# First products of a two-layer network: the making of their input chunks rewritten, norm sums reordered

## Chip, cores and metric

One Trainium2 chip, one core. The metric is the device time of one execution in microseconds, the median of several runs.

## What is computed

Two layers over 256 context and 256 latent tokens of width 1024, kept side by side as 512 columns. The modulation vectors come from `silu(cond) @ mod_w`, once with the latent's condition `c` and once with the context's. Cut to what the change touches:

```python
def ada_mod(cond, w, b):
    m = jax.nn.silu(cond) @ w + b
    return jnp.split(m[..., None, :], N_MOD, axis=-1)

mx = ada_mod(c, mod_w[i], mod_b[i]); mc = ada_mod(c_ctx, mod_w[i], mod_b[i])
x = x + 0.5 * mx[2] * swiglu(modulate(rms_norm(x, norm_g[i, 0]), mx[0], mx[1]),
                             ffn_w_in[i, 0], ffn_w_out[i, 0])      # the same for h_ctx with mc
# then a mixer (layer 0: gated linear recurrence, layer 1: retention), then a second swiglu
# modulate(h, shift, scale) = h * (1 + scale) + shift
```

At the end comes a last norm of the latent half alone.

## The kernel before

**Tiling.** Everything lies transposed: `x[k]` (k = 0..7) is a tile of 128 channels by 512 tokens, columns 0 to 255 context, 256 to 511 latent. The normed and modulated input of a product is `h[k]`, a high and a low part of 128x512 each (fp32r, a split of fp32 in two). Weights come as 371 tiles of 128x1024 (eight blocks of 128x128) in order of use; each is split by ScalarE (high part, L112) and VectorE (low part, L138). A block times a chunk is three matmuls (`mm3`, L142 to L144): high by high, high by low, low by high.

**Order.** The order of each engine's queue is that in which the program is written out (`manual_schedule`); an engine takes its queue in order. SP issues all transfers. Weight tiles are fetched up to four ahead and split two ahead of use (`w_ahead`, called from `w` at the first block of a tile; `w_low` emits the low part).

**Modulation.** `mods` lists 144 tiles of 128x1024, two vectors of 128 channels each (one for each condition). A tick (`_tick`) works off the next. In form V it is two VectorE multiplications with a sum (L242), in form P sixteen TensorE matmuls with two columns (L237). For layer 0, tiles 0, 2, 4, ... 14 are the shift of chunks 0 to 7 (form V), tiles 1, 3, ... 15 the scale (form P); `mod_finish` adds bias and norm gain in small VectorE steps (L262 to L265).

**Start.** `run` loads `cT`, `ident`, eight x tiles, two modulation tiles, the small vectors, then modulation and weight tiles in turn. Four fill matmuls (`warm`), then `spread_c` copies the conditions over all partitions with TensorE (L195). ScalarE squares the x tiles, VectorE adds them up (L286), `stat` (L296) sums over partitions on TensorE and computes the inverse root in ten small VectorE steps (L305 to L316), `bcast` (L329) spreads it. Tile 0 stands on VectorE between the sums and the ten steps, tile 1 on TensorE behind the sums, tiles 2 and 3 behind the broadcast. `h_chunk` makes an h: two VectorE steps (L346, one for each half), two ScalarE steps (L348), two VectorE steps for the low part (L354).

**First group.** `first_group` multiplies six column blocks (three pairs of the gated layer) by chunk 0, then by chunk 1 and so on, 18 matmuls for each chunk. A hook behind chunk k does the two ticks and the `h_chunk` of chunk k + 2. Behind chunk 7 comes `softplus_setup`, 29 small VectorE and two ScalarE steps. The gating (`post`, L485, L486, L157, L158) and the next pair of column blocks follow.

**The two ends with the latent half alone.** `boundary(x_only=True)` closes the retention and the last feed-forward layer: `out_proj` updates x chunk by chunk (L393) and squares it (`sq_acc`), VectorE adds the squares, then `stat`, ten fill matmuls, `bcast`, and, except at the very end, six more fill matmuls and two `h_chunk`s. The other four ends go half by half, with other products in between.

Of the kernel before, what the change touches and what calls it, by code (L numbers as in the profile page):

```python
# [9 lines left out]
F32 = mybir.dt.float32  # L10
# [6 lines left out]
P = 128  # L17
# [26 lines left out]
def mod_order():  # L44

    out = []
    for k in range(KD):
        out.append((0, 0, k, "V", True))
        out.append((0, 1, k, "P", True))
    for idx in range(2, 9):  # L50
        for k in range(KD):
            out.append((0, idx, k, "V", True))
    for idx in range(9):
        for k in range(KD):
            out.append((1, idx, k, "V", idx < 5))
    return out
# [18 lines left out]
class Kernel:  # L75
    def __init__(self, tc, aps):
        self.tc, self.nc, self.aps = tc, tc.nc, aps
        self.keys = []
        self.wt = {}
        self.raw = {}  # L80
        self.nsplit = 0
        self.wlow = deque()
        self.ndma = 0
        self.mods = mod_order()
        self.mod_done = 0
        self.mod_dma = 0
        self.mod_raw = {}
        self.mod_count = {}
        self.modpool = None
        self.hold = set()  # L90
        self.holdpool = None
        self.pend = []
        self.rate = 1
        self.bga, self.bgv = deque(), deque()

# [7 lines left out]

    def w_ahead(self, t):
        nc = self.nc
        self.w_fetch(min(t + LA + DA + 1, NTILES))
        while self.nsplit < min(t + LA + 1, NTILES):
            raw = self.raw.pop(self.nsplit)
            pool, tag = (self.holdpool, "h") if self.nsplit in self.hold else (self.wpool, "w")
            hi = pool.tile([P, BPT * P], F32R, tag=tag + "hi", name=tag + "hi", bufs=4)  # L110
            lo = pool.tile([P, BPT * P], F32R, tag=tag + "lo", name=tag + "lo", bufs=4)
            nc.scalar.activation(hi, raw, AF.Copy)  # L112
            self.wt[self.nsplit] = (hi, lo)
            self.wlow.append((lo, raw, hi))
            self.nsplit += 1

    def w(self, key, n=1):
# [6 lines left out]
        if o == 0:  # L124
            self.w_ahead(t)
            self.wt.pop(t - 2, None)
        if o >= 4 or t == 0:
            self.w_low()
# [97 lines left out]

    def _tick(self):
        nc = self.nc
# [5 lines left out]
        if form == "P":  # L234
            ps = self.psum()
            for kc in range(KD):
                nc.tensor.matmul(ps[:, 0:2], raw[:, kc * P:(kc + 1) * P], self.cT[:, kc, :],  # L237
                                 start=kc == 0, stop=kc == KD - 1)
            self.mod_finish(layer, idx, k, k + 1, 0, ps[:, 0:2])
        else:  # L240
# [11 lines left out]
    def mod_finish(self, layer, idx, k0, k1, c0, src=None):  # L252
        nc = self.nc
        m = self.M[layer][:, idx, k0:k1, c0:2]
        mb = self.vec("mb").rearrange("p (l i k c) -> p l i k c", l=2, i=9, k=KD)[:, layer, idx, k0:k1, c0:2]
        ng = self.vec("ng").rearrange("p (l i k c) -> p l i k c", l=2, i=3, k=KD)
        if src is None:
            src = m
        else:
            src = src.rearrange("p (k c) -> p k c", k=k1 - k0)[:, :, c0:2]  # L260
# [15 lines left out]
    def sq_acc(self, st, d, c0, c1):  # L276

        nc = self.nc
        w = c1 - c0
        if d == 0:  # L280
            acc = st["acc"] = self.tmp("acc")
            nc.scalar.activation(acc[:, :w], self.x[d][:, c0:c1], AF.Square)
        else:
            s = self.tmp("sq")
            nc.scalar.activation(s[:, :w], self.x[d][:, c0:c1], AF.Square)
            self.pend.append(lambda: nc.vector.tensor_tensor(st["acc"][:, :w], st["acc"][:, :w], s[:, :w],  # L286
                                                             ALU.add))

    def stat(self, s, ng, scale, between=None):


        nc = self.nc
        self.flush()
        ps = self.psum()
        for j in range(ng):
            nc.tensor.matmul(ps[:, j:j + 1], s[:, j * P:(j + 1) * P], self.ones, start=True, stop=True,  # L296
                             skip_group_check=True)
        if between:
            between()
        m = self.small.tile([P, 4], F32, tag="rs_m", name="rs_m")  # L300
# [58 lines left out]
    def out_proj(self, acts, key, layer, gidx, halves, st=None, hooks=None, tick=0, hold=False):  # L359
# [6 lines left out]
        for hi_, (c0, c1) in enumerate(halves):  # L366
# [14 lines left out]
            for d in range(KD):  # L381
# [6 lines left out]
                if st is not None and d:  # L388
                    self.sq_acc(st[hi_], d - 1, c0, c1)
                for c in range(2):  # L390
                    a0, a1 = max(c0, c * T), min(c1, (c + 1) * T)
# [12 lines left out]
    def boundary(self, acts, key, layer, gidx, nl, nn, x_only=False, hold=False):  # L404
# [3 lines left out]
        if x_only:  # L408
            st = [{}]
# [31 lines left out]

    def first_group(self, keys, x_only, hooks, ranges=None):

        hooks = hooks or {}
        banks = [self.psum() for _ in keys]
        held = {}
        for ri, (c0, c1) in enumerate(ranges or ([(T, 2 * T)] if x_only else [(0, T), (T, 2 * T)])):
            for k in range(KD):
# [12 lines left out]
        return banks  # L461

    def need_h(self, k, c0):
        if (k, c0) not in self.hdone:
            self.flush()
        assert (k, c0) in self.hdone, (k, c0)
# [8 lines left out]

    def ffn(self, layer, which, x_only, hooks, nl, nn, ranges=None, final=False, ticks=True):
        nc = self.nc
# [28 lines left out]
        phases = ((0, 5), (5, 10), (10, 15), (15, NF)) if x_only else PHASES  # L506
        NG = 3 if x_only or ranges else 2
        banks = self.first_group([col(f, g) for f in range(NG) for g in range(2)], x_only, hooks, ranges)
        if ticks:
# [459 lines left out]
    def run(self):  # L969
        nc, tc = self.nc, self.tc  # L970
        with ExitStack() as ctx:
# [46 lines left out]

            def h0(k):
                if k < KD:  # L1020
                    self.h_chunk(rb, 0, 0, k, 0, 2 * T)
                    self.flush()
            self.w_ahead(-LA)
            h0(0)
            self.w_low()

            def mk(k):
                def f():
                    if k + 2 < KD:
                        self._tick()  # L1030
                        self._tick()
                        h0(k + 2)
                    if k == KD - 1:
                        self.softplus_setup()
                return f
            self._tick()
            self._tick()
            h0(1)
            hooks = {(0, k): mk(k) for k in range(KD)}
            hooks = self.ffn(0, 0, False, hooks, 0, 1, ranges=[(0, 2 * T)])  # L1040
            hooks = self.lru(hooks)
# [135 lines left out]
```

## Time and profile before

| | us |
|---|---|
| median of 3 runs | 1887.81 (1887.64 to 1888.08) |
| the profiled execution | 1887.7 |
| its span | 1885.9 |
| TensorE busy | 1857.2 (98%) |
| VectorE busy | 1283.8 (68%) |
| ScalarE busy | 718.2 (38%) |
| mean granted TensorE clock | 0.991 |

Busy times are of the span. Matmuls overlap in the records, so a busy TensorE need not run at its peak; the granted clock says at which of its two levels it ran (1.00 is 2.4 GHz, 0.50 is 1.2 GHz). Times of rows are microseconds from the span's start.

### The profile page before, as it was taken

The numbers are of one execution on the slowest core, as the hardware profiler recorded it, in microseconds if no ns is written. First come the engines' busy times: TensorE is split into PE (matmuls) and PEld (weight loads), VectorE is DVE, ScalarE is ACT, GpSimd is POOL, SyncE is SP. The second block draws the span as 40 slices with busy tenths as digits, with TensorE's granted clock in tenths as the row PEclk, the third lists the DMA queues.
The fourth block names the chain that finished last, engine by engine and source line by source line (L and its number), as shares of the span: only waits on it lengthen the run. The fifth ranks groups of instructions, "written<-read, shape, count | busy, mean of one in ns | idle before, by whom it ended". The sixth has DMA issues, their size and how long they took to land.

```text
span 1885.9 us, 25731 instructions
## 1 busy us (share of the span) xinstructions
PE 1857.2 (98%) x10278; PEld 1621.5 (86%) x10278; DVE 1283.8 (68%) x2110; ACT 718.2 (38%) x984; POOL 0.2 (0%) x4
## 2 busy tenths in 40 slices
PE   8999999999999899999999999999999999999998
PEld 7888888897888888888889888888898899989997
DVE  7877697676899975767577655455576465675555
ACT  3322222248989342222224322222244243344442
POOL 0000000000000000000000000000000000000000
PEclk8999999999999999999999999999999999999999
DMA  8355454422322244454452445444324333355552
GB/s 319 127 211 187 167 189 181 145 90 79 100 90 90 79 157 168 158 185 172 143 172 94 154 150 187 145 171 178 102 80 150 124 123 118 97 160 182 176 186 101
DMA packets 77736, 277.52 MB, mean 147 GB/s; under 512 B 8752, under 2 KB 10032, under 8 KB 77616
## 3 DMA queue, kind: packets, MB, share of 16 engines
q1 hardware_dynamic: 77616, 275.88, 42.5%
q8 instruction: 80, 1.31, 0.3%
q14 instruction: 40, 0.33, 0.1%
HBM read 274.80 MB, written 1.05 MB: 146 GB/s over the span
## 4 chain that ended last, share of the span: by engine, by line
PE 92%; DVE 5%; ACT 1%; issue 1%; DMA 0%; SPq 0%; ACTq 0%; DVEq 0%
PE ps L142 30%; PE ps L144 30%; PE ps L143 30%; PE ps L237 1%; DVE x L393 1%; DVE wlo L138 1%; DVE hlo L138 1%; DVE h L354 0%; ACT h L348 0%; DVE acc L286 0%; PE ps L323 0%; PE ps L329 0%; PE ps L296 0%; DVE ht L346 0%; DMA x<-xt 0%
## 5 line engine op out<-in xcount | busy, mean ns | idle before, releaser
L142 PE MATMUL ps<-h,whi 128*128 128x512 f32 (+1 forms) x1824 | 641.1, 352 | 0.0
L144 PE MATMUL ps<-h,wlo 128*128 128x512 f32 (+1 forms) x1824 | 639.7, 351 | 1.2 <-DVE wlo L138 1.2
L143 PE MATMUL ps<-h,whi 128*128 128x512 f32 (+1 forms) x1824 | 640.3, 351 | 0.5 <-DVE h L354 0.5
L138 DVE TENSOR_TENSOR wlo<-wraw,whi 128x1024 fp32r<-128x1024 f32 x349 | 417.7, 1220 | 78.3 <-ACT whi L112 78.2
L112 ACT ACTIVATE whi<-wraw 128x1024 fp32r<-128x1024 f32 x349 | 357.3, 1050 | 275.8 <-PE ps L143 225.6
L144 PEld LDWEIGHTS ps<-h,wlo 128*128 128x128 f32 x1824 | 345.8, 190 | 47.7 <-DVE wlo L138 1.9
L143 PEld LDWEIGHTS ps<-h,whi 128*128 128x128 f32 x1824 | 345.9, 190 | 46.5 <-DVE h L354 1.6
L142 PEld LDWEIGHTS ps<-h,whi 128*128 128x128 f32 x1824 | 345.9, 190 | 44.9 <-ACT whi L112 0.3
L242 DVE SCALAR_TENSOR_TENSOR junk<-modraw,cB 128x1024 bf16<-128x1024 f32 x240 | 293.1, 1221 | 4.6
L393 DVE SCALAR_TENSOR_TENSOR x<-ps,M,x 128x256 f32<-128x256 f32 x296 | 132.5, 479 | 160.7 <-PE ps L144 160.3
L157 ACT ACTIVATE A<-sil 128x512 fp32r<-128x512 f32 (+1 forms) x88 | 50.9, 579 | 474.0 <-DVE sil L486 474.0
L142 PE MATMUL ps<-A,whi 128*128 128x512 f32 (+1 forms) x608 | 217.9, 358 | 0.0
L143 PE MATMUL ps<-A,whi 128*128 128x512 f32 (+1 forms) x608 | 217.9, 358 | 0.0
L144 PE MATMUL ps<-A,wlo 128*128 128x512 f32 (+1 forms) x608 | 217.9, 358 | 0.0
L486 DVE TENSOR_TENSOR sil<-ps,sil 128x512 f32<-128x512 f32 (+1 forms) x88 | 54.8, 623 | 159.8 <-PE ps L144 151.9
L144 PEld LDWEIGHTS ps<-A,wlo 128*128 128x128 f32 x608 | 114.9, 189 | 16.9
L143 PEld LDWEIGHTS ps<-A,whi 128*128 128x128 f32 x608 | 114.9, 189 | 16.9
L142 PEld LDWEIGHTS ps<-A,whi 128*128 128x128 f32 x608 | 114.9, 189 | 16.7
L158 DVE TENSOR_TENSOR A<-sil,A 128x512 fp32r<-128x512 f32 (+1 forms) x88 | 55.1, 626 | 56.7 <-ACT A L157 56.7
L485 ACT ACTIVATE sil<-ps 128x512 f32<-128x512 f32 (+1 forms) x88 | 47.3, 538 | 80.4 <-PE ps L144 79.9
L348 ACT ACTIVATE h<-ht,M 128x256 fp32r<-128x256 f32 x88 | 42.4, 504 | 91.5 <-DVE ht L346 91.5
L142 PE MATMUL ps<-A,hhi 128*128 128x256 f32 x192 | 54.8, 285 | 0.0
(171 smaller groups left out, 2065.3 us busy)
## 6 DMA issues: line engine op xcount, KB each, us to landing
wraw<-w SPq DMA_DIRECT2D x371, 512.0 KB, 4.3
modraw<-modw SPq DMA_DIRECT2D x144, 512.0 KB, 4.3
x<-xt SPq DMA_DIRECT2D x8, 256.0 KB, 4.9
mask<-mask SPq DMA_DIRECT2D x4, 512.0 KB, 6.0
out<-fin SPq DMA_DIRECT2D x8, 128.0 KB, 1.8
cs<-rope SPq DMA_DIRECT2D x1, 256.0 KB, 2.6
vecs<-vecs SPq DMA_DIRECT2D x1, 251.0 KB, 7.4
ident<-ident SPq DMA_DIRECT2D x1, 64.0 KB, 2.0
```

Of the source, the lines that this page charges most:

```text
L112: nc.scalar.activation(hi, raw, AF.Copy)
L138: self.nc.vector.tensor_tensor(lo, raw, hi.bitcast(F32), ALU.subtract)
L142: mm(ps, whi, xhi, start=first, stop=False, skip_group_check=True)
L143: mm(ps, whi, xlo, start=False, stop=False, skip_group_check=True)
L144: mm(ps, wlo, xhi, start=False, stop=last, skip_group_check=True)
L157: self.nc.scalar.activation(hi, src, AF.Copy)
L158: self.nc.vector.tensor_tensor(lo, src, hi.bitcast(F32), ALU.subtract)
L242: nc.vector.scalar_tensor_tensor(self.junk, raw, 1.0, self.cB[:, c, :], op0=ALU.mult, op1=ALU.mult, accum_out=M[:, idx, k, c:c + 1])
L348: nc.scalar.activation(h[:, 0, a:b], tt, AF.Identity, bias=M[:, 3 * n, k, c:c + 1])
L393: nc.vector.scalar_tensor_tensor(self.x[d][:, a0:a1], ps[:, a0 - c0:a1 - c0], M[:, gidx, d, c:c + 1], self.x[d][:, a0:a1], op0=ALU.mult, o ...
L485: nc.scalar.activation(s[:, :w], pa[:, c0:c1], AF.Silu)
L486: nc.vector.tensor_tensor(s[:, :w], pg[:, c0:c1], s[:, :w], ALU.mult)
```

## The change

The shift of chunk 0 (tile 0) becomes form P. `stat` takes no function to run in between any more; both tiles of chunk 0 are emitted around it, their small steps (`late`) behind the ten steps. Seven fill matmuls follow `spread_c`, three stand before the broadcast. The start's products go through a new `start_group`: the work for chunk k + 1 (two ticks, the new way of making h, one weight tile's split) is emitted behind the first of chunk k's six blocks, and transfers are issued there, modulation first. The new way makes `xr = x * rb` on VectorE, scale and shift on ScalarE (two halves), the high part by a copy on ScalarE, the low part by one VectorE subtraction of 512 columns. Scale's two small steps become one. Automatic splitting of weights is off in this group. In all `out_proj` with sums, the addition of the last square is emitted ahead of the update of x instead of behind it; at the two latent ends the last square is not added but summed by TensorE as a second part, and the ten fill matmuls are six.

```diff
-        out.append((0, 0, k, "V", True))
+        out.append((0, 0, k, "V" if k else "P", True))
...
+        if src is not None and idx == 1:
+            nc.vector.tensor_scalar(m[:, 0], src, self.mb1[:, k0:k0 + 1], ng[:, layer, 0, k0, 0:1], op0=ALU.add,
+                                    op1=ALU.mult)
+            return
...
+            if d == KD - 1 and st.get("two"):
+                st["last"] = s
+                return
...
-            y = self.stat(st[0]["acc"], 2, 1.0 / D)
-            self.warm(10)
+            y = self.stat([st[0]["acc"], st[0]["last"]], 2, 1.0 / D)
+            self.warm(6)
...
                     self.sq_acc(st[hi_], d - 1, c0, c1)
+                    self.flush()
...
+    def start_group(self, rb, keys):
+        nc = self.nc
+        M = self.M[0]
+        banks = [self.psum() for _ in keys]
+        splits = (2, 3, 4, 4, 5, 6, 7, 8)
+        for k in range(KD):
+            for n, (b, key) in enumerate(zip(banks, keys)):
+                whi, wlo = self.w(key(k))
+                self.mm3(b, whi, wlo, self.h[k][:, 0], self.h[k][:, 1], k == 0, k == KD - 1)
+                if n or k + 1 == KD:
+                    continue
+                h = self.h[k + 1] = self.hpool.tile([P, 2, 512], F32R, tag="h", name="h%d" % (k + 1), bufs=KD)
+                xr = self.tmp("xr")
+                nc.vector.tensor_tensor(xr, self.x[k + 1], rb, ALU.mult)
+                self.mod_prefetch(min(2 * k + 10, 2 * KD), True)
+                self.w_fetch(k + 5)
+                self._tick()
+                self._tick()
+                t = self.tmp("ht")
+                for c in range(2):
+                    nc.scalar.activation(t[:, c * T:(c + 1) * T], xr[:, c * T:(c + 1) * T], AF.Identity,
+                                         bias=M[:, 0, k + 1, c:c + 1], scale=M[:, 1, k + 1, c:c + 1])
+                nc.scalar.activation(h[:, 0], t, AF.Copy)
+                self.w_split(splits[k])
+                nc.vector.tensor_tensor(h[:, 1], t, h[:, 0].bitcast(F32), ALU.subtract)
+                self.w_low()
+        self.w_split(splits[-1])
+        self.w_low()
+        self.softplus_setup()
+        self.auto = True
+        return banks
...
             todo = self.spread_c()
+            self.warm(7)
             st = {}
             for k in range(KD):
                 self.sq_acc(st, k, 0, 2 * T)
-            self.flush()
+                self.flush()
             for o, ps in todo:
                 nc.scalar.activation(o, ps, AF.Copy)
-            y = self.stat(st["acc"], 4, 1.0 / D, self._tick)
-            self._tick()
+            late = []
+            self._tick(late)
+            y = self.stat(st["acc"], 4, 1.0 / D)
+            self._tick(late)
+            self.warm(3)
             rb = self.bcast(y, 4)
...
-            self.w_ahead(-LA)
-            h0(0)
+            self.auto = False
+            self.w_split(1)
+            self.h_chunk(rb, 0, 0, 0, 0, 2 * T)
+            self.flush()
             self.w_low()
...
-            hooks = self.ffn(0, 0, False, hooks, 0, 1, ranges=[(0, 2 * T)])
+            hooks = self.ffn(0, 0, False, lambda keys: self.start_group(rb, keys), 0, 1)
```

## Rows read from the trace of the kernel before

**Rows 1.** The page's chain that ended last, shares of the span by engine.

```profile
PE 92%; DVE 5%; ACT 1%; issue 1%; DMA 0%; SPq 0%; ACTq 0%; DVEq 0%
```

**Rows 2.** windows: stretch, length, busy time (instructions) by engine, granted clock, DMA share, GB/s.

```profile
10.00:12.00 2.00, 0.00 (x0) 0.00 (x0) 1.69 (x4) 1.96 (x4) 0.00 (x0) 0.88 1.01 411
```

**Rows 3.** timeline: start, length, engine, line, operation, count [idle before <- releaser].

```profile
3.36 4.44 PE L195 MATMUL ps<-ident,cT 128*128 128x128 f32 x32 [0.26 <-DMA ident<-ident]
```

**Rows 4.** chain piece by piece, from the start: start, length, engine, tile, line.

```profile
12.47 1.86 PE ps L296 x8
...
17.75 1.92 PE ps L329 x8
...
22.87 0.64 PE ps L142
...
28.20 0.43 PE ps L142
...
28.89 0.23 PE ps L144
...
31.49 0.34 PE ps L142
...
61.11 0.35 PE ps L142
```

**Rows 5.** source line L212, first modulation transfer: issue, and time to landing.

```profile
L212 SPq DMA_DIRECT2D modraw<-modw x1: 430/430/430, 5.4 to 5.4; - x1
...
DMA to landing us min/median/max: 6.4/6.4/6.4
```

**Rows 6.** timeline of VectorE and ScalarE, 19 to 31 us.

```profile
19.70 0.87 DVE L346 SCALAR_TENSOR_TENSOR ht<-x,M,ps 128x256 f32<-128x256 f32 x2 [1.56 <-PE ps L329]
...
22.69 1.22 DVE L242 SCALAR_TENSOR_TENSOR junk<-modraw,cB 128x1024 bf16<-128x1024 f32 x1
...
25.22 0.16 DVE L265 TENSOR_TENSOR M<-M,vecs 128x2 f32<-128x2 f32 x1
...
26.20 0.91 ACT L348 ACTIVATE h<-ht,M 128x256 fp32r<-128x256 f32 x2 [5.08 <-DVE ht L346]
...
27.02 1.99 ACT L112 ACTIVATE whi<-wraw 128x1024 fp32r<-128x1024 f32 x2
...
28.09 2.36 DVE L138 TENSOR_TENSOR wlo<-wraw,whi 128x1024 fp32r<-128x1024 f32 x2 [0.46 <-ACT whi L112]
```

**Rows 7.** timeline of VectorE, behind the first group.

```profile
65.72 0.17 DVE L945 SCALAR_TENSOR_TENSOR spt<-vecs 128x20 f32<-128x20 f32 x1
...
71.53 0.68 DVE L486 TENSOR_TENSOR sil<-ps,sil 128x512 f32<-128x512 f32 x1
72.92 0.69 DVE L158 TENSOR_TENSOR A<-sil,A 128x512 fp32r<-128x512 f32 x1 [0.70 <-ACT A L157]
```

**Rows 8.** chain piece by piece, last end of the latent half.

```profile
1873.78 0.44 DVE acc L286
...
1874.87 3.87 PE ps L323 x10
1878.73 0.46 PE ps L329 x4
```

**Rows 9.** timeline, the same end.

```profile
1874.26 0.61 PE L296 MATMUL ps<-ones,acc 128*128 128x1 f32 x4 [1.54 <-DVE acc L286]
...
1876.68 0.16 DVE L316 SCALAR_TENSOR_TENSOR rs_y<-rs_t,rs_y 128x2 f32<-128x2 f32 x1
```

**Rows 10.** windows of 1 us, the same end.

```profile
1875.00:1876.00 1.00, 1.00 (x5) 0.32 (x4) 0.83 (x6) 0.00 (x0) 0.00 (x0) 0.60 0.00 0
```

**Rows 11.** chain piece by piece, the latent end behind the retention.

```profile
1679.31 0.87 PE ps L329 x4
```

**Rows 12.** timeline, the same end.

```profile
1677.98 0.16 DVE L316 SCALAR_TENSOR_TENSOR rs_y<-rs_t,rs_y 128x2 f32<-128x2 f32 x1
...
1684.67 0.38 PE L143 MATMUL ps<-h,whi 128*128 128x256 f32 x1 [0.47 <-DVE h L354]
```

More of the change, by code (lines that the diff above doesn't have):

```diff
@@ L104, in w_ahead, with w_split @@
     def w_ahead(self, t):
+        self.w_fetch(min(t + LA + DA + 1, NTILES))
+        self.w_split(min(t + LA + 1, NTILES))
+    def w_split(self, n):
         nc = self.nc
-        self.w_fetch(min(t + LA + DA + 1, NTILES))
-        while self.nsplit < min(t + LA + 1, NTILES):
+        while self.nsplit < n:
             raw = self.raw.pop(self.nsplit)
@@ L124, in w @@
         if o == 0:
-            self.w_ahead(t)
+            if self.auto:
+                self.w_ahead(t)
             self.wt.pop(t - 2, None)
-        if o >= 4 or t == 0:
+        if self.auto and o >= 4:
             self.w_low()
@@ L225, in tick, with _tick @@
             self._tick()
-    def _tick(self):
+    def _tick(self, late=None):
         nc = self.nc
@@ L238, in _tick @@
                                  start=kc == 0, stop=kc == KD - 1)
-            self.mod_finish(layer, idx, k, k + 1, 0, ps[:, 0:2])
+            f = lambda: self.mod_finish(layer, idx, k, k + 1, 0, ps[:, 0:2])
+            f() if late is None else late.append(f)
         else:
@@ L285, in sq_acc, with stat @@
             nc.scalar.activation(s[:, :w], self.x[d][:, c0:c1], AF.Square)
+            if d == KD - 1 and st.get("two"):
+                st["last"] = s
+                return
             self.pend.append(lambda: nc.vector.tensor_tensor(st["acc"][:, :w], st["acc"][:, :w], s[:, :w],
                                                              ALU.add))
-    def stat(self, s, ng, scale, between=None):
+    def stat(self, s, ng, scale):
         nc = self.nc
@@ L294, in stat @@
         ps = self.psum()
+        parts = s if isinstance(s, list) else [s]
         for j in range(ng):
[L296 to L299, printed above, removed]
+            for i, s in enumerate(parts):
+                nc.tensor.matmul(ps[:, j:j + 1], s[:, j * P:(j + 1) * P], self.ones, start=i == 0,
+                                 stop=i == len(parts) - 1, skip_group_check=True)
         m = self.small.tile([P, 4], F32, tag="rs_m", name="rs_m")
@@ L408, in boundary @@
         if x_only:
-            st = [{}]
+            st = [{"two": True}]
             self.out_proj(acts, key, layer, gidx, [(T, 2 * T)], st=st)
-            y = self.stat(st[0]["acc"], 2, 1.0 / D)
-            self.warm(10)
+            y = self.stat([st[0]["acc"], st[0]["last"]], 2, 1.0 / D)
+            self.warm(6)
             rb = self.bcast(y, 2)
@@ L440, in boundary, with first_group @@
                 (1, 1): lambda: hc(1, 6), (1, 2): lambda: hc(1, 7)}
-    def first_group(self, keys, x_only, hooks, ranges=None):
+    def first_group(self, keys, x_only, hooks):
         hooks = hooks or {}
@@ L446, in first_group @@
         held = {}
-        for ri, (c0, c1) in enumerate(ranges or ([(T, 2 * T)] if x_only else [(0, T), (T, 2 * T)])):
+        for ri, (c0, c1) in enumerate([(T, 2 * T)] if x_only else [(0, T), (T, 2 * T)]):
             for k in range(KD):
@@ L461, in first_group @@
         return banks
+    def start_group(self, rb, keys):
[27 more added lines that the diff above has]
+        self.softplus_setup()
+        self.auto = True
+        return banks
     def need_h(self, k, c0):
@@ L473, in proj, with ffn @@
         return ps
-    def ffn(self, layer, which, x_only, hooks, nl, nn, ranges=None, final=False, ticks=True):
+    def ffn(self, layer, which, x_only, hooks, nl, nn, ticks=True):
         nc = self.nc
@@ L506, in ffn @@
         phases = ((0, 5), (5, 10), (10, 15), (15, NF)) if x_only else PHASES
-        NG = 3 if x_only or ranges else 2
-        banks = self.first_group([col(f, g) for f in range(NG) for g in range(2)], x_only, hooks, ranges)
+        start = callable(hooks)
+        NG = 3 if x_only or start else 2
+        keys = [col(f, g) for f in range(NG) for g in range(2)]
+        banks = hooks(keys) if start else self.first_group(keys, x_only, hooks)
         if ticks:
@@ L1010, in run @@
                 self.sq_acc(st, k, 0, 2 * T)
-            self.flush()
+                self.flush()
             for o, ps in todo:
                 nc.scalar.activation(o, ps, AF.Copy)
-            y = self.stat(st["acc"], 4, 1.0 / D, self._tick)
-            self._tick()
-            rb = self.bcast(y, 4)
-            self.h, self.hdone = [None] * KD, set()
[L1019 to L1022, printed above, removed]
-            self.w_ahead(-LA)
-            h0(0)
-            self.w_low()
[L1027 to L1039, printed above, removed]
-            hooks = self.ffn(0, 0, False, hooks, 0, 1, ranges=[(0, 2 * T)])
+            late = []
[3 more added lines that the diff above has]
+            self.warm(3)
+            rb = self.bcast(y, 4)
+            self.mb1 = self.const.tile([P, KD], F32, name="mb1")
+            mb = self.vec("mb").rearrange("p (l i k c) -> p l i k c", l=2, i=9, k=KD)
+            nc.vector.tensor_scalar(self.mb1, mb[:, 0, 1, :, 0], 1.0, None, op0=ALU.add)
+            for f in late:
+                f()
+            self.h, self.hdone = [None] * KD, set()
+            self.auto = False
+            self.w_split(1)
+            self.h_chunk(rb, 0, 0, 0, 0, 2 * T)
+            self.flush()
+            self.w_low()
+            hooks = self.ffn(0, 0, False, lambda keys: self.start_group(rb, keys), 0, 1)
             hooks = self.lru(hooks)
```

## Prediction, made before the changed kernel ran

> **What bounds the kernel now.** The page's chain comes first: of the work that ended last TensorE carries 92% [rows 1], so a part of the change is worth something only where TensorE waits or is slow. Second come windows of 2 us: from 10 to 12 the granted clock is 0.88 [rows 2], that is, TensorE drops from 2.4 to 1.2 GHz near 11.5, having been idle since 7.8 [rows 3]. Third is the chain piece by piece [rows 4]: norm sums at 12.47 for 1.86, modulation tile 1 on TensorE from 14.33 to 17.75 (3.41), broadcast (1.92), tile 3 from 19.67 to the first product at 22.87 (3.2). Products take 0.43 until 28.4 and 0.23 from 28.9: almost six microseconds of dense products pass before the clock is full. From there TensorE is never idle in the first group: chunk 1's first product stands at 31.49, chunk 6's at 61.11, so (61.11 - 31.49)/5 = 5.92 per chunk, which is 18 products of 0.228 and a tile of 1.8. Chunks 6 and 7 have 36 products and no tile, so the group ends at 61.11 + 0.1 + 36 x 0.228 = 69.4. That is the number to beat. VectorE works beside it with few waits, two chunks ahead. Last come the two ends where only the latent half is normed, near 1674 and 1873.
>
> The profiled execution took 1887.7 for a span of 1885.9; the median is 1887.81. I add to 1887.7.
>
> **The new prelude.** Tile 0 of the modulation moves from VectorE to TensorE, and in TensorE's queue it stands ahead of the norm sums. Its transfer is issued at 5.43 and lands 6.4 later, at 11.85 [rows 5]; the squares' sum is there at 12.42. So the sums, now at 12.47, wait for a tile that cannot begin before 11.85, and behind them wait the ten small VectorE steps, the broadcast and every h. The order on TensorE becomes tile 0, sums, tile 1, three fill matmuls, broadcast. At half clock, with the rows' prices: 11.85 + 3.4 + 1.86 + 3.41 + 3 x 0.43 + 1.92 = 23.7. At full clock, with about half of each: 1.9, 1.0, 1.9, 0.65 and 1.1; the broadcast waits for VectorE's small steps (2.0 behind the sums) and ends near 18.4. Which clock? Seven fill matmuls behind the first products fill 7.8 to 9.3, then TensorE idles until 11.85, then come sixteen products of two columns. Rows show such two-column tiles from 14.3 to 17.7 and 19.7 to 22.9 without a rise [rows 4]. I let the clock be at half from 13.0, between 11.5 as now and not at all: tile 0 ends 14.5, sums 16.4, tile 1 19.8, fill 21.1, broadcast 23.0 (bounds 18.4 and 23.7). Now it ends at 19.67. In return tile 3 leaves this place (3.2 us), so the first product comes about 1.4 behind the broadcast (two VectorE steps of 0.87 together, then ScalarE's [rows 6]): 24.4, against 22.87.
>
> The Trainium skill, "TensorE: Matmul & The Clock Gate", section "What's actually happening", says that "the default state is throttled, and activity releases the throttle"; read simply, the fill matmuls would hold 2.4 GHz through the prelude, which is the second rival below. The trace agrees only in part, as the two-column tiles of [rows 4] passed at half clock without releasing anything.
>
> **The new chunk loop.** Now VectorE makes chunk k+2 while TensorE multiplies k. In the change it makes chunk k+1, in one serial loop: xr from PSUM, 128x512, 0.68 [rows 7]; both halves of the modulation tile, 25.22 - 22.69 = 2.53; two small steps, 0.27; then it waits for ScalarE: two 256-wide steps in 0.91 and a 512-wide copy [rows 6], of which the like is 0.70 of waiting in front of a low part [rows 7], so 1.6 in all; then its low part, 0.69; and, behind that, the low part of a weight tile (1.18 each, 2.36 for two), which waits again because ScalarE starts the tile's high part (1.0 each, 1.99 for two) only after that copy [rows 6]. VectorE takes its queue in order, so nothing fills these waits: the next xr and the next modulation tile stand behind them. The weight's high part ends some 2.6 behind the two small steps, its low part at 3.85. Sum: 0.68 + 2.53 + 0.27 + 3.85 = 7.3, less 0.2 since consecutive VectorE steps overlap a little (0.87 for two of 0.48): 7.1 for a chunk with a weight tile, 5.6 without. Of the seven rounds only the fourth is without. Busy time alone would be 5.3, under TensorE's 5.92; it is the waits for ScalarE that make 7.1.
>
> Step by step, from the broadcast at 23.0: h0 ready 24.4, the low part of weight tile 0 at +3.1 = 26.1; third product 26.1; tile 3 at half clock until 29.9; 15 products at 0.43 [rows 4], the last few perhaps faster, until 36.0. VectorE needs tile 3's sums: its small steps end at 30.1, h1 at 31.7, VectorE free at 34.0. TensorE begins chunk 1 at 36.0 and has tile 5 at 38.6, for which VectorE waits; small steps done 38.8. From here VectorE leads: four rounds of 7.1 and one of 5.6 put the last small steps at 72.8, the high part of h7 at 74.4, its low part at 75.0, and 17 products of 0.23 end the group at 78.9. Against 69.4 that is 9.5 later. TensorE, which loses chunks 0 and 1 to the half clock, catches up and then waits up to one microsecond per chunk from chunk 4 on.
>
> Behind the group VectorE still has one weight tile and the softplus (now from 65.7 to 71.5, 5.8 [rows 7]). It is free some 4.7 behind TensorE's group, where it is 2.1 behind now. The next 48 products (10.9 us) have their weights already; the low part that the ones behind them need comes 5.5 after the softplus (two gated tiles, 4.3, and 1.2), at 10.2. I cost it at nothing; if that cover is gone, 1 to 2 us.
>
> **The two ends.** At 1874 TensorE does ten fill matmuls, 3.87 us from 1874.87, so the broadcast starts at 1878.73 [rows 8], though the last small VectorE step had ended at 1876.84 [rows 9]: the fill is on the path. With six, and without the last addition (0.44 [rows 8]; the added TensorE steps give back about 0.2), the sums end near 1874.65, the small steps 1876.6, the fill 1876.6; the broadcast at half clock (clock 0.60 in that microsecond [rows 10]) takes 0.9 instead of 0.46 and ends at 1877.55 instead of 1879.19. Gain 1.6, between 1.2 and 2.1. At 1676 the same ten keep the broadcast until 1679.31 [rows 11], while the small steps end at 1678.14 [rows 12]: 1.2, and 0.2 from the sums, so it comes 1.4 earlier. But six more fill matmuls behind it hold the first product, so that I give it 0.5 of this at once, and 0.47 where a product now waits for a low part at 1684.67 [rows 12]: 1.0, between 0.3 and 1.5.
>
> **Costed at nothing.** Additions put ahead of the residual updates: ScalarE has the square of one block while TensorE still multiplies the next, so the addition is over when the update's products end; if it weren't, an update would be late by 0.44 at most, and other banks are free. Transfers reordered on SP: now weight transfers that wait for a buffer stand ahead of modulation tiles 8 and 9 in that queue; in the change these two are first used in the loop's fourth round, past 45, while a landing took 6.4 [rows 5]. If one landed late, its chunk would lose just that. One VectorE pair and some small steps fewer: VectorE waits there.
>
> **Sum.** 1887.7 + 9.5 - 1.6 - 1.0 = 1894.6 us, 0.36% slower.
>
> **Rivals.**
> (1) The chain is hidden and it is faster: had VectorE a round of at most 5.92, TensorE would set the pace at full clock from the first product. It speaks for it that the busy time is only 5.3 and that products at half clock now cost about 2.6 (13 of them at 0.43 instead of 0.23); against it, the three hand-overs to ScalarE in a row, and that ScalarE's part would have to take 0.4 and not 1.6. With the broadcast at 18.4: 1.4 + 1.2 (weight) + 45.4 (144 products, 7 tiles) gives 66.4, 3.0 earlier than now; with the ends' 2.6: 1882.1.
> (2) The fill holds the clock through the prelude, the loop stays at 7.1. Broadcast 18.4, VectorE's loop from 21.5: first small steps done 25.0, five rounds of 7.1 and one of 5.6 to 66.1, 2.3 to the last low part, 3.9 of products: 72.3, 2.9 later than now; less 2.6: 1888.0, no change that can be told.
> (3) The clock falls again inside the group. At 1875 it fell after 1.5 us without work, some one-column matmuls and the first fill [rows 9, 10]; from chunk 4 on, a wait, three products and a two-column tile follow each other in the same way. Chunks at half clock would cost 18 x 0.2 + 1.6 = 5.2 more each, less the microsecond that TensorE waits anyway; one to two such chunks add 4 to 8: about 1900.
> (4) That the kernel doesn't do what the change says: I see no part without effect.
>
> **Numbers.** Chances: forecast 0.57 (1891 to 1898: 2.7 below and 0.7 above for a broadcast between 20.3 and 23.7, 0.9 each way for the ends, 2 above for VectorE's lag), (1) 0.12, (2) 0.20, (3) 0.11. A difference under about 0.2% (3.8 us) can't be told from none. Faster 0.10; same 0.23, from (2) and the edges; slower 0.67. The range takes in the forecast, (2) down to 1886 and the lower half of (3): 1886 to 1899.
>
> **What would show it.** Broadcast of the first norm ends after 21; granted clock 0.50 across it. On VectorE, first xr to next xr 7.1 with two idle stretches before the low parts, both ended by ScalarE. TensorE idle before the first product of chunks 4 to 7. Group end near 79. At 1875 the broadcast starts as soon as the last small step ends. I am wrong if a chunk comes every 5.9 us, if the sums stand before 14, or if the clock is full at the first product.

## The result, and the profile after

The changed kernel takes 1905.6 us (median; 1904.5 to 1908.2), the kernel before 1887.7 beside it (1884.9 to 1888.1): a ratio of 1.010, 95% interval 1.0082 to 1.0117. The forecast was 1894.6, between 1886 and 1899. The sign was right and the size was not: slower by some two and a half times what had been worked out (17.9 instead of 6.9). In later measurements the kernel before has medians of 1885.4 to 1885.9 (single executions from 1883.0 to 1889.2). Set against those, the change costs some 20 us, an estimate across measurements, and the 1887.7 from which the sum started was one of the longer executions.

The page of the changed kernel, busy time by engine and the chain that ended last:

```profile
span 1902.7 us, 25702 instructions
...
PE 1867.5 (98%) x10304; PEld 1629.2 (86%) x10304; DVE 1279.2 (67%) x2083; ACT 723.6 (38%) x991; POOL 0.2 (0%) x4
...
PE 86%; DVE 9%; ACT 3%; issue 1%; DMA 0%; SPq 0%; ACTq 0%; DVEq 0%
```

TensorE has nearly the same matmuls to do (10304 records against 10278). In the chain its share fell from 92% to 86% [rows 1], and VectorE and ScalarE together rose from 6% to 12%: there are more places where TensorE stands still for them, and the next question is where.

A mark that every norm has tells that: the first of the ten small steps (start of the first `rs_m` step, from the timelines of VectorE). How much later than in the kernel before each kernel reaches it, in us. The columns are named by the time of that step in the kernel before; 389 to 1375 are the first steps of the four ends that go half by half, 1643 is the last of the retention's own norms, 1676 and 1875 belong to the two latent ends (the experiments in the other rows follow below):

| | 389 | 643 | 1009 | 1375 | 1643 | 1676 | 1875 | span |
|---|---|---|---|---|---|---|---|---|
| after | 10.5 | 13.9 | 16.6 | 18.4 | 20.1 | 19.9 | 18.4 | 16.8 |
| e1, additions behind again | 11.9 | 11.9 | 11.9 | 11.9 | 12.0 | 11.8 | 10.4 | 8.8 |
| e2, additions ahead, alone | 0.9 | 3.3 | 6.0 | 7.8 | 9.2 | 9.2 | 7.9 | 6.4 |
| e3, start alone | 12.3 | 12.2 | 12.2 | 12.2 | 12.3 | 12.3 | 12.6 | 11.0 |
| e5, additions ahead, of an older square | -0.9 | -1.1 | -1.1 | -1.0 | -0.8 | -0.8 | -2.1 | -2.0 |

Each row is one execution. e5 has the start of the kernel before and still reaches 389 earlier by 0.9, so differences of about 1 us between rows can come from the execution alone.

The first group ends at 78.3 in the trace after, 8.9 later than the 69.4 of before; the forecast had 9.5 there. But the lag grows on at each of the four ends that the forecast had cost at nothing. At the first of them, the timeline of VectorE, ScalarE and TensorE after (start, length, engine, line, operation, count [idle before <- releaser]):

```profile
392.74 1.22 DVE L143 TENSOR_TENSOR wlo<-wraw,whi 128x1024 fp32r<-128x1024 f32 x1
...
393.87 0.42 DVE L301 TENSOR_TENSOR acc<-acc,sq 128x256 f32<-128x256 f32 x1
...
394.21 0.48 DVE L409 SCALAR_TENSOR_TENSOR x<-ps,M,x 128x256 f32<-128x256 f32 x1
...
394.78 0.42 ACT L297 ACTIVATE sq<-x 128x256 f32<-128x256 f32 x1 [0.50 <-DVE x L409]
...
395.23 0.42 DVE L301 TENSOR_TENSOR acc<-acc,sq 128x256 f32<-128x256 f32 x1 [0.55 <-ACT sq L297]
...
395.57 0.48 DVE L409 SCALAR_TENSOR_TENSOR x<-ps,M,x 128x256 f32<-128x256 f32 x1
...
398.94 0.61 PE L313 MATMUL ps<-ones,acc 128*128 128x1 f32 x4 [1.35 <-DVE acc L301]
...
399.58 0.16 DVE L320 TENSOR_SCALAR rs_m<-ps 128x2 f32<-128x2 f32 x1 [0.30 <-PE ps L313]
```

The last line is the mark of the table. The same timeline of the kernel before:

```profile
386.54 0.48 DVE L393 SCALAR_TENSOR_TENSOR x<-ps,M,x 128x256 f32<-128x256 f32 x1
...
387.11 0.42 ACT L285 ACTIVATE sq<-x 128x256 f32<-128x256 f32 x1 [1.44 <-DVE x L393]
...
387.29 0.48 DVE L393 SCALAR_TENSOR_TENSOR x<-ps,M,x 128x256 f32<-128x256 f32 x1
...
388.53 0.50 PE L296 MATMUL ps<-ones,acc 128*128 128x1 f32 x4
```

None of these updates waits for TensorE: their products were done before, and VectorE is in arrears. Before, it goes from one update to the next in 387.29 - 386.54 = 0.75, since ScalarE squares while VectorE goes on. After, the addition of the newest square stands ahead of the next update, so such a round is update, square, addition, one behind the other: 395.57 - 394.21 = 1.36. Where the low part of a weight tile happens to stand between update and addition, as at 392.74, the addition (393.87) doesn't wait: the square is made meanwhile. The sums come late and TensorE waits 1.35 for them, where it waited for nothing. Then its clock drops. Windows of the trace after (stretch, length, busy time with instructions of PE, PEld, DVE, ACT, POOL, granted clock, DMA share, GB/s); the granted clock was 1.00 in all windows of these stretches of the kernel before:

```profile
400.00:405.00 5.00, 5.00 (x32) 5.00 (x31) 2.91 (x12) 0.79 (x2) 0.00 (x0) 0.66 0.02 6
656.00:660.00 4.00, 3.99 (x20) 3.99 (x21) 2.65 (x13) 0.42 (x1) 0.00 (x0) 0.57 0.25 100
```

The start, TensorE's timeline after:

```profile
11.91 1.95 PE L243 MATMUL ps<-cT,modraw 128*128 128x2 f32 x16 [1.17 <-DMA modraw<-modw]
13.72 1.12 PE L313 MATMUL ps<-ones,acc 128*128 128x1 f32 x8
14.71 3.55 PE L243 MATMUL ps<-cT,modraw 128*128 128x2 f32 x16
...
19.36 1.92 PE L344 MATMUL ps<-ident,rs_y 128*128 128x128 f32 x8
22.78 0.49 PE L147 MATMUL ps<-h,whi 128*128 128x512 f32 x1 [1.51 <-ACT h L363]
...
24.77 3.40 PE L243 MATMUL ps<-cT,modraw 128*128 128x2 f32 x16
...
77.95 0.39 PE L149 MATMUL ps<-h,wlo 128*128 128x512 f32 x1
```

Tile 0 waits for its transfer until 11.91 (forecast 11.85), and the sums for tile 0. The clock falls near 14.5 (the window from 14 to 16 has 0.63), between one and two microseconds later than forecast, so the broadcast ends at 21.28, not 23.0. It is full again for a moment at the first product (0.49), which the forecast had excluded, and at half once more in tile 3 (3.40). The sums stand at 13.72, where it had 14.5. The last line is the group's last product; its end is the 78.3. VectorE's loop behind the broadcast, one round, after:

```profile
39.95 0.68 DVE L494 TENSOR_TENSOR xr<-x,ps 128x512 f32<-128x512 f32 x1
...
43.16 0.27 DVE L265 TENSOR_SCALAR M<-ps,mb,vecs 128x2 f32<-128x2 f32 x1
45.25 0.69 DVE L505 TENSOR_TENSOR h<-ht,h 128x512 fp32r<-128x512 f32 x1 [1.82 <-ACT h L503]
46.20 1.23 DVE L143 TENSOR_TENSOR wlo<-wraw,whi 128x1024 fp32r<-128x1024 f32 x1 [0.26 <-ACT whi L116]
47.35 0.68 DVE L494 TENSOR_TENSOR xr<-x,ps 128x512 f32<-128x512 f32 x1
```

From xr to xr 47.35 - 39.95 = 7.40, with two stretches of idle time ahead of the low parts, both ended by ScalarE, as forecast (7.1; the wait 1.82 instead of 1.6). TensorE has 5.92 of work in a chunk and waits. In two stretches of the group its clock falls again (windows after, columns as above):

```profile
50.00:55.00 5.00, 5.00 (x25) 4.15 (x23) 3.14 (x8) 1.72 (x3) 0.00 (x0) 0.79 0.07 30
70.00:75.00 5.00, 5.00 (x19) 3.94 (x18) 2.88 (x6) 3.43 (x5) 0.00 (x0) 0.74 0.19 75
```

The last latent end, after:

```profile
1892.42 0.38 PE L313 MATMUL ps<-ones,sq 128*128 128x1 f32 x2 [0.96 <-ACT sq L297]
...
1893.11 1.46 PE L338 MATMUL ps<-warm_sb 128*128 128x512 bf16 x6
...
1895.28 0.71 PE L344 MATMUL ps<-ident,rs_y 128*128 128x128 f32 x4 [0.71 <-DVE rs_y L331]
```

The six fill matmuls (1.46, where ten took 3.87 [rows 8]) are over before the last small step, and the broadcast waits for that step, as forecast.

### The profile page after: what moved, and what is told of

Its sections match the earlier page's. It is cut to its first block, busy times and chain, and to the rows that moved or that the text cites. A ratio compares the mean times of both kernels' runs of the same rounds, so it can differ in the third digit from the quotient of the medians.

```text
span 1902.7 us, 25702 instructions
## 1 busy us (share of the span) xinstructions
PE 1867.5 (98%) x10304; PEld 1629.2 (86%) x10304; DVE 1279.2 (67%) x2083; ACT 723.6 (38%) x991; POOL 0.2 (0%) x4
## 4 chain that ended last, share of the span: by engine, by line
PE 86%; DVE 9%; ACT 3%; issue 1%; DMA 0%; SPq 0%; ACTq 0%; DVEq 0%
PE ps L149 28%; PE ps L148 28%; PE ps L147 28%; DVE wlo L143 1%; DVE x L409 1%; DVE hlo L143 1%; DVE acc L301 1%; DVE junk L249 1%; ACT sq L297 1%; ACT h L363 1%; ACT hhi L116 1%; PE ps L243 1%; DVE h L369 1%; DVE ht L361 0%; ACT whi L116 0%
## 5 line engine op out<-in xcount | busy, mean ns | idle before, releaser
L147 PEld LDWEIGHTS ps<-A,whi 128*128 128x128 f32 x608 | 114.9, 189 | 16.8
L149 PEld LDWEIGHTS ps<-A,wlo 128*128 128x128 f32 x608 | 114.9, 189 | 16.8
L297 ACT ACTIVATE sq<-x 128x256 f32<-128x256 f32 (+1 forms) x77 | 33.4, 434 | 69.2 <-DVE x L409 67.4
L363 ACT ACTIVATE h<-ht,M 128x256 fp32r<-128x256 f32 x74 | 36.0, 504 | 58.3 <-DVE ht L361 56.9
```

The source lines that it names most:

```text
L147: mm(ps, whi, xhi, start=first, stop=False, skip_group_check=True)
L149: mm(ps, wlo, xhi, start=False, stop=last, skip_group_check=True)
L363: nc.scalar.activation(h[:, 0, a:b], tt, AF.Identity, bias=M[:, 3 * n, k, c:c + 1])
```

## Experiments

**The additions.** The theory from the trace after: the early additions, not the start, cost what the forecast lacked. e2 puts them alone into the kernel before, e1 takes them out of the kernel after.

e2, on the kernel before (in `out_proj`):

```diff
                 if st is not None and d:
                     self.sq_acc(st[hi_], d - 1, c0, c1)
+                    self.flush()
```

> The kernel before with that one line alone: the addition ahead of the update. Theory: 4 ends at 2.8 us each, so 1887.7 + 11.2 = 1898.9; at the two latent ends it gains or loses under 0.5. Rival (late start): no change, 1887.7.

Measured: 1895.4 (1892.3 to 1897.1), ratio 1.0052 (1.0035 to 1.0068), 10.0 us over the 1885.5 of the kernel before in the same measurement; less than the 1898.9 expected, but far from no change.

e1, on the kernel after:

```diff
                     self.sq_acc(st[hi_], d - 1, c0, c1)
-                    self.flush()
```

> The changed kernel with one line undone: in the column blocks that also square x, the addition of the last square stands behind the update of x again. Theory: the trace of the changed kernel stands 8.9 us behind at the end of the first group, 20.1 behind the four two-half ends, and 16.8 at its own end; the 11.2 in between come from VectorE, which is late at these ends, waiting for each square before it may do the next update. This kernel then takes 1905.6 - 11.2 = 1894.4, as the first forecast said (1894.6). Rival: the 11.2 come from VectorE and the transfers being late behind the new start; then the line does nothing and this takes 1904 to 1906.

Measured: 1895.8 (1893.5 to 1896.5), ratio 1.0052 (1.0037 to 1.0067): 9.8 less than the kernel after, which was measured at another time (with each set against the kernel before beside it, 17.9 - 10.3 = 7.6 less). In the table above its lag is 11.9 at the first end and 11.9 still at the fourth, while that of e2 grows by 1.3 to 2.7 from one mark to the next, up to 9.2. The waits of VectorE grouped (engine, line, waited for: us in total, times, longest) show the same without any timeline. In the kernel after:

```profile
DVE acc L301 <- ACT sq L297: 24.3, 35, 4.7
```

The same group in e1:

```profile
DVE acc L301 <- ACT sq L297: 9.2, 6, 4.8
```

And in e2:

```profile
DVE acc L286 <- ACT sq L285: 25.6, 37, 4.7
```

In the kernel before the same group has 9.6 us in 9 waits. The one line makes 28 to 29 more waits, of about half a microsecond each. TensorE's waits for the sums, in the kernel before:

```profile
PE ps L296 <- DVE acc L286: 9.6, 8, 4.7
```

And in e2:

```profile
PE ps L296 <- DVE acc L286: 14.3, 11, 3.4
```

The longest of each is the one at the start; without it 4.9 have become 10.9. So TensorE's waits carry some 6 of the 10 us. What a wait does at the second end that goes half by half, TensorE's timeline of e2:

```profile
645.45 0.82 PE L296 MATMUL ps<-ones,acc 128*128 128x1 f32 x4 [2.26 <-DVE acc L286]
...
647.56 0.41 PE L142 MATMUL ps<-Y,whi 128*128 128x256 f32 x1
647.77 0.41 PE L143 MATMUL ps<-Y,whi 128*128 128x256 f32 x1
```

and the same place in the kernel before:

```profile
642.38 0.61 PE L296 MATMUL ps<-ones,acc 128*128 128x1 f32 x4 [0.71 <-DVE acc L286]
...
644.01 0.28 PE L142 MATMUL ps<-Y,whi 128*128 128x256 f32 x1
644.13 0.28 PE L143 MATMUL ps<-Y,whi 128*128 128x256 f32 x1
```

The wait is 1.55 longer, and behind it the products stand 0.21 apart instead of 0.12, as at half clock. The granted clock of e2 is 0.66 from 645 to 650 and again from 1382 to 1387, behind the sums of the fourth end; behind those of the first and third it stays at 1.00. By an estimate, 0.34 of 5 us twice, that is 3.4 of the 10.

e5 asks whether it is the place of the addition or the wait in it. On the kernel before, the addition stands ahead of the update too, but it is that of the square two chunks back, which is there by then:

```diff
                 if st is not None and d:
+                    self.flush()
                     self.sq_acc(st[hi_], d - 1, c0, c1)
...
-                self.flush()
+                if st is None:
+                    self.flush()
```

> The kernel before with the addition ahead of the update of x, as in the changed kernel, but of the square before the last: ahead of the update of chunk d stands the addition of chunk d-2, whose square ScalarE has long made. Theory: what costs 10 us is that VectorE waits for the square just emitted, a round of update, square, addition in 1.36 us where 0.73 was enough; here nothing waits, so as the kernel before of this call (1885.5 in the last one), within 1. Rival: an addition ahead of the update costs by its place (0.4 more before each update); then some 1888 to 1895.

Measured: 1885.6 (1885.1 to 1887.1), ratio 0.9995 (0.9985 to 1.0004). VectorE waits 4 times for squares, 6.3 us in all. So an addition directly ahead of an update costs nothing when its square is there. This rules out less than it seems: in the kernel before, too, updates and additions alternate on VectorE, and ahead of an update stands the addition of the square two chunks back; e5 only moves the weights' low parts and other steps that fall between them. It is close to a repetition of the kernel before. That the wait costs, rather than the place, rests on the waits counted above.

**The start alone.** e3 is the kernel after with the early additions and both latent-end edits undone:

```diff
-                    self.flush()
...
-            st = [{"two": True}]
+            st = [{}]
...
-            y = self.stat([st[0]["acc"], st[0]["last"]], 2, 1.0 / D)
-            self.warm(6)
+            y = self.stat(st[0]["acc"], 2, 1.0 / D)
+            self.warm(10)
```

> The changed kernel with both edits of the ends undone, so the new start alone. Theory: 8.9 us, the lag at the end of the first group, and nothing behind it: 1896.6. Rival: the late start costs further at every end, 1905 to 1908.

Measured: 1897.8 (1896.9 to 1899.4), ratio 1.0065 (1.005 to 1.008): 12.3 over the kernel before, and in its trace the lag is 12.2 to 12.3 from the end of the first group on and doesn't grow up to the latent ends. So the start costs 12.3 in the median, though the trace of the kernel after shows only 8.9. The difference is the clock: from 12 to 82 the mean granted clock is 0.85 in the trace after and 0.80 in that of e3, and 0.05 of 70 us is 3.5, an estimate that fits the 3.4 between the two. It begins with tile 0, whose sixteen matmuls take 1.95 in the trace after, at full clock, 3.15 in that of e3 and 3.58 in that of e1, of which this is TensorE's timeline:

```profile
11.78 3.58 PE L243 MATMUL ps<-cT,modraw 128*128 128x2 f32 x16 [2.47 <-DMA modraw<-modw]
15.21 1.84 PE L313 MATMUL ps<-ones,acc 128*128 128x1 f32 x8
...
21.57 1.92 PE L344 MATMUL ps<-ident,rs_y 128*128 128x128 f32 x8
```

There TensorE had been idle 2.47 before tile 0, after only 1.17, and the broadcast ends at 23.49 instead of 21.28.

**What in the start.** e6 is e1 with the weight tile's split written into VectorE's wait: ScalarE starts the tile's high part ahead of its steps for h, and VectorE makes the low part of the weight while ScalarE works on h.

```diff
                 self._tick()
                 self._tick()
+                self.w_split(splits[k])
...
                 nc.scalar.activation(h[:, 0], t, AF.Copy)
-                self.w_split(splits[k])
-                nc.vector.tensor_tensor(h[:, 1], t, h[:, 0].bitcast(F32), ALU.subtract)
                 self.w_low()
+                nc.vector.tensor_tensor(h[:, 1], t, h[:, 0].bitcast(F32), ALU.subtract)
```

> e1_add_behind (1895.8) with one step moved in the new start's loop: the weight tile's high part on ScalarE ahead of the chunk's steps, its low part on VectorE inside the wait for ScalarE. Theory: the loop of 7.4 us is VectorE's waits in a row; this takes it to about 5.9, that is TensorE's own pace, and the group ends 3 to 5 earlier: 1891 to 1893. Rival: the start loses its time to the half clock of chunks 0 and 1, and the loop is hidden behind that; then 1895 to 1896.

Measured: 1888.4 (1886.2 to 1891.7), ratio 1.0013 (1.0004 to 1.0023): 7.4 less than e1. VectorE's timeline of e6:

```profile
42.05 0.27 DVE L265 TENSOR_SCALAR M<-ps,mb,vecs 128x2 f32<-128x2 f32 x1
42.25 1.22 DVE L143 TENSOR_TENSOR wlo<-wraw,whi 128x1024 fp32r<-128x1024 f32 x1
44.16 0.69 DVE L505 TENSOR_TENSOR h<-ht,h 128x512 fp32r<-128x512 f32 x1 [0.69 <-ACT h L503]
44.76 0.68 DVE L493 TENSOR_TENSOR xr<-x,ps 128x512 f32<-128x512 f32 x1
```

Of the idle time of 1.82 and 0.26 only 0.69 is left in this round. In TensorE's timeline the tiles start at 40.16 and 46.09, 5.93 apart, which is its own work; the granted clock is 1.00 from 36 to the end of the group, at 73.4. So the wait for ScalarE, not VectorE's work, had made the round, and with the round go the falls of the clock inside the group. The time lies below the 1891 to 1893 expected. Of the 7.4 a part may be the execution: the broadcast ends at 21.1 in the trace of e6 and at 23.5 in that of e1. Against the trace after, where it also ended early (21.28), the group ends some 5 us sooner (73.4 against 78.3), as expected.

e7 is e1 with tile 0 on VectorE again, where it stood before (form V, between the sums and the ten small steps):

```diff
-        out.append((0, 0, k, "V" if k else "P", True))
+        out.append((0, 0, k, "V", True))
...
-            self._tick(late)
-            y = self.stat(st["acc"], 4, 1.0 / D)
+            y = self.stat(st["acc"], 4, 1.0 / D, self._tick)
```

> e1_add_behind with tile 0 of the modulation on VectorE again, between the sums and the ten small steps as in the kernel before; fills and loop stay. Theory: the sums come at 12.5 instead of 13.7 to 15.2, the broadcast ends between 18.9 and 21 instead of 21.3 to 23.5, and VectorE's loop behind it carries that 1 to 1: 1892.5 to 1894.5. Rival: the group's end is set by when the clock comes back; then 1895 to 1896.5.

Measured: 1892.6 (1892.1 to 1894.1), ratio 1.0034 (1.0022 to 1.0046): 3.1 less than e1. The sums start at 12.48 and the broadcast at 18.85, 2.7 earlier than in e1. As expected, 1892.5 to 1894.5. The loop is as slow as in e1, and its clock falls as it did after (0.63 from 48 to 52, 0.69 from 68 to 72).

e9 has both edits, those of e6 and of e7.

> Part e6 (a weight tile's split inside the wait for ScalarE) and part e7 (tile 0 on VectorE again) together, on the kernel after without its early additions. The theory has two separate terms at the start: a late broadcast, and a round of 7.4 us. If they add, the time is the 1895.8 of e1 less 7.4 (e6) and less 3.1 (e7): 1885.3, which is before's own time (ratio 1.000), though the latent ends in it are worth 1.75; the first stretch then still costs some 1.5 us against before. The small steps at the first two-half end stand near 390 (389.1 in before, 393.1 in e6, 398.1 in e7). Rival: the two overlap, since with a 5.9 us round TensorE sets the pace and an earlier broadcast only makes VectorE lead more: 1887 to 1888.5, small steps near 392 to 393. Second rival: with both gone the new chain is better than the old one, as TensorE leaves half clock earlier: 1884 or less, small steps before 389.

Measured: 1888.5 (1886.8 to 1888.9), ratio 1.0013 (1.0003 to 1.0022). The forecast of 1885.3 failed; the two gains don't add. In its trace the group ends at 71.6, 1.8 before that of e6, but the medians of the two are the same (the profiled execution of e9 was 1.7 below its median), so what tile 0 costs once the round fits lies between nothing and 1.8. That trace's first product comes two microseconds before that of the kernel before, and its group still ends 2.2 later. Windows of e9:

```profile
24.00:28.00 4.00, 4.00 (x16) 3.71 (x17) 3.02 (x7) 1.05 (x2) 0.00 (x0) 0.50 1.03 407
28.00:32.00 4.00, 4.00 (x14) 3.15 (x13) 3.23 (x5) 1.62 (x3) 0.00 (x0) 0.69 1.03 411
```

TensorE is at half clock until 30.4, against 28.6 in the trace of the kernel before and 26.3 in that of e5: with the tile of the next chunk behind the first three products, the dense products start later (26.4 against 22.7) although the first one comes earlier. That this is what remains of the start's cost is read from the trace; no run changes it alone.

**The latent ends.** e4 puts their edits alone into the kernel before (the last square summed by TensorE, six fill matmuls, additions ahead of the update there alone):

```diff
+            if d == KD - 1 and st.get("two"):
+                st["last"] = s
+                return
...
                     self.sq_acc(st[hi_], d - 1, c0, c1)
+                    if st[hi_].get("two"):
+                        self.flush()
...
-            self.warm(10)
+            self.warm(6)
```

> The kernel before with the two latent ends changed alone: last square summed by TensorE, six fill matmuls, addition ahead of the update in these two only. Theory: the lag fell by 1.5 at the first and 1.6 at the last, so 1887.7 - 3.2 = 1884.5. The forecast had 2.6, 1885.1. Rival: part of that gain was slack given back from what was lost before; then 1886 to 1887.

Measured: 1883.7 (1883.1 to 1884.9), ratio 0.9991 (0.9982 to 1.0001), an interval that just takes in no change. By medians that is 1.75 less than the kernel before, by traces 1885.9 - 1882.5 = 3.4. The ten fill matmuls, which become six, cost different amounts in different executions. e2 has the same fill there as the kernel before. TensorE's timeline of the kernel before:

```profile
1874.73 4.00 PE L323 MATMUL ps<-warm_sb 128*128 128x512 bf16 x10
```

And in e2:

```profile
1882.64 2.32 PE L323 MATMUL ps<-warm_sb 128*128 128x512 bf16 x10
```

In e2 the clock stays full through the fill, which is then 1.7 shorter, and that much less is to be gained. The traces of e3 (2.32) and e5 (4.00) are one of each. At the first latent end the ten take 3.29 before and 3.94 in e3, but 2.32 in e2 and e5. So the forecast was made from an execution in which the fill ran at half clock at both ends, and the median gain is smaller because that is not always so; how often, no run counts.

**A dense fill.** e8 is e4 with 21 fill matmuls behind `spread_c` and six ahead of the first broadcast, to see whether the first stretch at half clock can be bought off:

```diff
             todo = self.spread_c()
+            self.warm(21)
...
             self._tick()
+            self.warm(6)
             rb = self.bcast(y, 4)
```

> The kernel before with the latent ends (1883.7) and a fill that leaves no hole: 21 matmuls behind the first products of the start instead of none, so that TensorE works until the norm sums, and six ahead of the broadcast. Theory: it is the idle 4.7 us before the sums that cost the clock; with it gone the first product comes up to 2.9 earlier and 13 products don't run at 0.43: 1879 to 1881. Rival: the two-column tiles let the clock fall anyway; then 1883 to 1885.

Measured: 1883.5 (1882.6 to 1884.8), ratio 0.9986 (0.9976 to 0.9995), the fastest kernel here, but 0.2 from e4, which can't be told from nothing. The 1879 to 1881 expected failed, and the rival's 1883 to 1885 held. Windows of e8:

```profile
12.00:16.00 4.00, 4.00 (x32) 3.28 (x31) 3.69 (x10) 2.12 (x5) 0.00 (x0) 1.00 1.03 410
16.00:20.00 4.00, 3.92 (x18) 2.74 (x15) 1.75 (x11) 0.68 (x1) 0.00 (x0) 0.57 1.03 410
20.00:24.00 4.00, 4.00 (x17) 3.81 (x17) 3.78 (x8) 0.91 (x2) 0.00 (x0) 0.50 1.03 407
```

The fill keeps the clock at 1.00 until 16. Then, behind the one-column sums and a two-column tile, it falls all the same, at about the six further fill matmuls, while the record shows TensorE busy 3.92 of 4 us. The first product comes at 22.70, as in the kernel before (22.73).

## Why the prediction was off, step by step

The three edits alone add up to the whole, as far as it is known: +12.3 (e3), +10.0 (e2) and -1.75 (e4) make +20.5; 1905.6 less the 1885.5 of the kernel before in their measurement is +20.1, less the 1887.7 beside it +17.9.

- **Additions ahead of the updates: the step that failed.** It was costed at nothing, because ScalarE was to have "the square of one block while TensorE still multiplies the next". Where it came out so, nothing was lost: at the latent end at 1676 the lag of e2 stays at 9.2. At the four ends in two halves VectorE is itself behind TensorE's products, so the update that feeds the square is just over, and the wait is a full round trip. The bound given, "an update would be late by 0.44 at most", priced the addition's own length; it is the wait ahead of the addition that costs, 1.36 for a round instead of 0.75, and it adds up over the blocks until TensorE waits for the sums and, at some ends, falls to half clock. Measured: 10.0 alone (e2), 9.8 when taken out (e1; 7.6 by the measurements beside each), nothing with the older square (e5). Without this line the kernel (e1) takes 1895.8, near the 1894.6 forecast, but in part by luck, because errors cancel: the base was 2.2 too high (1887.7 against 1885.5), the start 2.8 too low, and the gain at the ends 0.85 too large; 1894.6 - 2.2 + 2.8 + 0.85 = 1896.05.
- **The start, +9.5: right in mechanism, short in size.** Tile 0's transfer, the sums behind it, the round of 7.1 (7.40 measured) and its two waits for ScalarE stand in the trace as described; e6 shows that the round was a large part, since 7.4 of the 12.3 go with it by medians, some 5 by the traces with like broadcasts. What stays in e6 is 4.3 (2.55 above the kernel before beside it, and the 1.75 of its latent ends); e7 and e9 don't take it apart further. The trace after has +8.9, the median +12.3 (e3). The forecast put the clock's fall at one point between the bounds, and executions differ in just that. Two of its three signs of being wrong came true in the trace after, sums before 14 (13.72) and full clock at the first product, and in e3 the second again, while the serial loop, the larger term, stood; the repeated fall inside the group, the third rival, stands in the traces of after (0.79 and 0.74 above), e1 (0.66 from 60 to 64), e3 (0.50 from 72 to 76) and e7, so it belonged in the likeliest case.
- **The latent ends, -2.6: right in mechanism, too large.** Measured -1.75 (e4, its interval just taking in none), as ten fill matmuls cost 4.00 in some executions and 2.32 in others, and the profiled one was of the first kind.
- **The softplus behind the group, costed at nothing ("1 to 2 us" if uncovered):** the lags of e1 and e3 stay the same to 0.1 from the group's end to the norm at 389, so nothing is lost there. The transfers' new order shows no wait of its own: from 19 to 82 in the traces of after and e1 no wait of TensorE, VectorE or ScalarE ends with a transfer.
- **Rivals.** The first (the loop hidden, 1882) is refuted by the round of 7.40; and e6, whose round is 5.93, still took 1888.4, so a round that fits doesn't give 1882 either. The second (the fill holds the clock, 1888) is refuted in every trace of the new start: the clock is at half before the broadcast. The Trainium skill, "TensorE: Matmul & The Clock Gate", section "What's actually happening", cited there with it, says that activity releases the throttle. That fits e8 only as far as the dense fill goes: at 16 to 20 there was activity, and the clock fell.

## What to carry to other kernels

Before an operation is moved ahead of another in an in-order queue, look whether its engine is in arrears there: if the steps around it don't wait for the engine that feeds them, every operand made by another engine from the last result is a full round trip, and the older operand is the free one (the kernel before, and e5). A wait that can't be removed should hold work that is there anyway: the weight's low part in the wait for ScalarE gave back 5 to 7.4 of 12.3 us (e6), and at the two-half ends the additions behind such a low part waited for nothing. And a term read from one execution next to a change of clock should carry both prices of the row, 2.32 and 4.00 here.

## What was not expected of the hardware

The same instructions at the same place ran at either level of the clock from one execution to the next: ten fill matmuls in 2.32 or 4.00 us, tile 0 in 1.95 (after), 3.15 (e3) or 3.58 (e1). And in e8 the granted clock went from 1.00 (12 to 16) to 0.57 (16 to 20) with TensorE's records idle for 0.08 us in that window, behind one-column and two-column fp32 matmuls; 4.7 us of dense fill shortly before did not prevent it.
